# Decoder layer on one core: the values from the unshifted x in the first pass, the index queries in the second

## The chip, the cores and the metric

The kernel runs on one core of one Trainium2 chip. TensorE (PE) multiplies, VectorE (DVE) and ScalarE (ACT) work element by element, GpSimd (POOL) and SyncE (SP) here issue nearly nothing but transfers (DMA). The metric is the device time of one execution in microseconds (us); lower is better.

## The reference

One decoder layer on x of 512 tokens x 2048 channels, with a condition c of 2048 numbers. What matters here:

```python
mod = silu(c) @ w_ada + b_ada                     # 6 x 2048 numbers
sh1, sc1, gt1, sh2, sc2, gt2 = split(mod, 6)
h = rmsnorm(x, g_mix) * (1 + sc1) + sh1
proj = h @ w_in       # q_a k_a v_a, q_b k_b v_b, qi, ki, wi, g_a, g_b
y_a = stick_breaking_attention(q_a, k_a, v_a) @ w_a         # 8 heads
y_b = dsa_attention(rope(q_b), rope(k_b), v_b, rope(qi), rope(ki), wi) @ w_b
x = x + (1 + gt1) * ((sigmoid(g_a) * y_a + sigmoid(g_b) * y_b) @ w_o)
h = rmsnorm(x, g_ffn) * (1 + sc2) + sh2
x = x + (1 + gt2) * conv_ffn(h, w_up, conv_w, conv_b, w_down)
return rmsnorm(x, g_final)
```

v_a has 1024 columns, qi 1024 (16 heads of 64). The norm of a token is one number, 1/rms, so for the unshifted s = x * g_mix * (1 + sc1) one has h = s / rms + sh1 and h @ w = (s @ w) / rms + sh1 @ w.

## The kernel before

Every large product is made of three fp32r matmuls of a high and a low half (`mm3`, L178 to L180: high by high, high by low, low by high). Weights come by SP into a ring of 8 tiles `raw` (`load`, L153 to L155); ACT makes their high half `wh` (L168), DVE the low half `wl` (L170), in three rooms. x and h are cut into 16 tiles of 128 channels (KT), counted by k. Tiles of 128x512 come from a ring of 62 (`slot`, named F), small working tiles from pairs named `w`, `T`, `ta`, `sp`, and one tile of 128x1280 is named `soft`. PSUM has three `acc` banks, four `att` and one `outs`. Each engine runs its instructions in a fixed order, which a scheduler made from the code; `behind(...)` pins an instruction after another.

mod is made in 160 halves (`ada_half`): a load of 512 KB of w_ada by SP (L320) and a product with a sum on DVE (L321, 128x1024). They are strewn over the program.

Pass 1 (loop at L397) makes 7 of the 8 query tiles from s: in each of 16 steps two halves of sc1, one tile of x, its square for the norm (L394), s in high and low (ACT, and DVE at L418), one weight tile and 21 matmuls of 512 columns. In its last step come the norm: four pairs of small matmuls (L368), the root, the spread over all partitions (L379) and its copy (L424). Pass 2 (L463) makes, in each of 16 steps, h of tile k (L437, L438, cast L466, low half L468), two halves of sh1 for the next tile, and 24 matmuls into eight tiles of values. Behind it come the tail columns (ki, wi), the eighth query tile (`w_qi7`) from h, and two tiles of the other columns.

Since the seven query tiles lack the shift and the norm, these come later. 31 units (`unit`, 168 matmuls of 256 columns each, a Strassen-like product of 2 x 2 blocks) make the other columns. In each, `between` is called twice and advances the tasks of `beside` by a step: tables of the rotary functions, `shift_queries` (sh1 @ w_qi, from w_qiT on DVE at L610, with diagonal matrices spread by PE at L596), and `index_ropes` (for each query tile: load, times 1/rms at L647, plus the shift at L648, rotary), and after these halves of mod in `soft`, one in a step. A second half of mod is taken in each unit at the second call. In the stick-breaking heads, `some_ada(2)` stands in each head. The units of w_o (u = 0 to 7) take one half of mod each, and behind u = 6 `some_ada(len(ada_left))` issues whatever is left of the 160. L1104 to L1112 are in that loop; the last unit (u = 7) has the second norm's work in it. Then come the units of w_up and w_down.

Of the kernel before, what the change touches and what calls it, by code (L numbers as in the profile page):

```python
# [10 lines left out]
F32 = mybir.dt.float32  # L11
# [65 lines left out]
def block_kernel(ctx: ExitStack, tc: tile.TileContext, A: dict, out: bass.AP):  # L77
# [284 lines left out]
    def rms(squares, blocks=range(NQB), bank=outs):  # L362

        total = bank()
        at = slice(blocks[0] * P, (blocks[-1] + 1) * P)
        for b in blocks:
            for i, t in enumerate(squares):
                mm(total[:, b : b + 1], t[:, b * P : (b + 1) * P], ones[:, :1], start=b == blocks[0] and i == 0,  # L368
                   stop=i == len(squares) - 1, skip_group_check=True)
        r = sb.tile([P, NQB], F32, tag="r", bufs=2, name=nm("r"))  # L370
        rb = r[:, blocks[0] : blocks[-1] + 1]
        act(rb, total[:, blocks[0] : blocks[-1] + 1], AF.Sqrt, scale=1.0 / D, bias=eps)
        nc.vector.reciprocal(rb, rb)
# [5 lines left out]
        mm(out[:, at], ones, wide[:, at], start=True, stop=True)  # L379
        yield out  # L380


    xt, total = [], None
    qi_ps = [acc() for _ in range(3)] + [att() for _ in range(4)]
    norm = None

    def next_x():
        x = slot()
# [5 lines left out]
            tt(total, total, sq, ALU.add)  # L394
        return total or sq

    for k in range(KT):  # L397
        if k == 6:
            past = t2k("w", 2)[:, :P]
            with behind(pins["load"]):  # L400
                nc.sync.dma_start(const, A["consts"][:, :5])
                nc.sync.dma_start(past, A["consts"][:, 5])
            nc.gpsimd.tensor_copy(mask[0], ident)
            nc.gpsimd.tensor_copy(mask[1], past)
# [6 lines left out]
        if k == KT - 1:  # L411
            norm = rms([total])
            next(norm)
        ada_end(t, t + 1)
        stt(amp[:, 0, k : k + 1], mod[:, t : t + 1], 1.0, g_mix[:, k : k + 1], ALU.add, ALU.mult)
        h0 = slot(F32R), slot(F32R)
        act(h0[0], x, AF.Copy, scale=amp[:, 0, k : k + 1])
        stt(h0[1], x, amp[:, 0, k : k + 1], h0[0].bitcast(F32), ALU.mult, ALU.subtract)  # L418
        w = prep(A["w_qi"][k], NQ * P)
        for j in range(NQ):  # L420
            mm3(qi_ps[j], cols(w, j), h0, k == 0, k == KT - 1)
            if k == KT - 1 and j == 0:
                rstd = t2k("T", 2)
                act(rstd, next(norm), AF.Copy)  # L424
# [30 lines left out]
    pv = None

    def ada_tile(k):
        last = [ada_half(cb, k, half) for half in range(2)][1]
        ada_end(k, k + 1)
        return last  # L460

    ada_tile(0)
    for k in range(KT):  # L463
        modulate(xt[k], k, 0, xt[k])
        hi, lo = slot(F32R), slot(F32R)
        act(hi, xt[k], AF.Copy)  # L466
# [10 lines left out]
        for i in range(8):  # L477
            mm3(pv[i], cols(h[k], i % 4), cols(w, i // 4, S), k == 0, k == KT - 1)
        if k in EARLY:
            forms_late(EARLY.index(k))  # L480
    for i in range(8):
        save(vd[i], evac(pv[i]))
# [12 lines left out]
    save(td_tail[:TN], evac(ps, slice(0, TN))[:TN])  # L495

    xd = dram("xd", 64)
    for j, (src, dst) in enumerate(((A["w_qi7"], qid[7]), (A["w_x0"][0], xd[0]), (A["w_x0"][1], xd[1]))):
        ps = (acc, att)[j % 2]()
        for c in range(2):  # L500
            w = prep(src[c])
            for k in range(8):
                i = 8 * c + k
                last = mm3(ps, cols(w, k), h[i], i == 0, i == KT - 1)
                if j == 2 and k % 2:
# [78 lines left out]
            save(rope_d[n], o)  # L584

    rope_d = dram("rope", 2, 2 * S)
    corr = macc[:, : 2 * NQ, :].rearrange("p (j a) b -> p j (a b)", a=2)

    def shift_queries():

        rows = [t2k(tag, 2) for tag in ("w", "T") for _ in range(2)]
        diag = None
        for i in range(5):
            if i:
                ps = outs()
                mm(ps, ones, diag, start=True, stop=True)  # L596
                act(rows[i - 1], ps, AF.Copy)
            if i < 4:
                diag = t2k("ta", 2)
                for b in range(4):  # L600
                    ts(diag[:, b * P : (b + 1) * P], ident, mod[:, 4 * i + b : 4 * i + b + 1], None, ALU.mult)
                yield
        for j in range(NQ):
            for half in range(2):
                w = sb.tile([P, 1024], F32, tag="soft", name=nm("soft"))
                nc.sync.dma_start(w, A["w_qiT"][j, :, half * 1024 : (half + 1) * 1024])
                for i in range(2):
                    at = w[:, i * S : (i + 1) * S]
                    n = 2 * half + i
                    stt(at, at, 1.0, rows[n], ALU.mult, ALU.mult, accum_out=corr[:, j, n : n + 1])  # L610
                yield
        tt(corr[:, :, :2], corr[:, :, :2], corr[:, :, 2:], ALU.add)
        tt(corr[:, :, 0], corr[:, :, 0], corr[:, :, 1], ALU.add)
# [18 lines left out]
    def index_ropes():  # L632

        tabs = [t2k("T", 2) for _ in range(2)]
        for i, t in enumerate(tabs):
            save(t, rope_d[1][:, i * S : (i + 1) * S])
        rstd = t2k("w", 2)
        save(rstd, rd)
        for j in range(9):
            r = t2k("w", 2)  # L640
            soft = sb.tile([P, 10 * P], F32, tag="soft", name=nm("soft"))
            tmp = soft[:, :S], soft[:, S : 2 * S]
            if j < 8:
                save(r, qid[j])
                yield
                if j < NQ:
                    tt(r, r, rstd, ALU.mult)  # L647
                    act(r, r, AF.Identity, bias=corr[:, j, 0:1])  # L648
                    yield
# [233 lines left out]
    for hd in range(NH):  # L883
# [632 lines left out]
def _layout(i):  # L1516
# [102 lines left out]
```

## Time and profile before

| | |
|---|---|
| Times of three runs | 2747.16, 2744.15, 2747.07 us (median 2747.07) |
| Profiled execution | 2744.77 us, of which the span is 2742.9 (1.87 us lie around it) |
| PE busy | 2678.6 us, 98% of the span |
| DVE busy | 2409.0 us, 88% |
| ACT busy | 1450.6 us, 53% |
| POOL busy | 314.2 us, 11% |
| Mean granted clock of PE | 0.995 |

Pass 1 lies at 13.5 to 98 us, pass 2 at 101.6 to about 190, the units from 236 to 860, the stick heads from 905 to about 1100, the units of w_o from 1247 to 1411. A row of a timeline gives start and length in us, engine, line, operation, what it writes and reads with shapes, and in brackets how long the engine had been idle and what ended that. A row of waits gives who waited for whom, the sum in us, how many times, and the longest.

### The profile page before, as it was taken

To read this page: it belongs to the slowest core of one execution; us is meant where nothing else is said; L and a number is where in the kernel's file an instruction comes from. 1 tells how busy PE (TensorE), PEld (TensorE's weight loads), DVE (VectorE), ACT (ScalarE), POOL (GpSimd) and SP (SyncE) were. 2 spreads that over 40 slices of the span, in tenths; PEclk is the share of its full clock that TensorE was granted. 3 is DMA by queue.
4 is the path that set the end of the run, shared out by engine and by line. 5 is a ranking of instruction groups with operands and counts; after the bars stand their busy time and mean duration, and the time that the engine had idled before them with its cause. 6 is when DMAs were issued, how large, how long until landed. Compare 5 with 4: busy or idle time off the path is not lost. (4 is left out here: it accounts for less than half of the span.)

```text
span 2742.9 us, 47708 instructions
## 1 busy us (share of the span) xinstructions
PE 2678.6 (98%) x18704; PEld 2449.0 (89%) x18704; DVE 2409.0 (88%) x3452; ACT 1450.6 (53%) x2045; POOL 314.2 (11%) x519
## 2 busy tenths in 40 slices
PE   8999999999999999999999999999999999999996
PEld 6779999999998777889999999999999998888875
DVE  8978989988897899788888999999999997888876
ACT  4444454455556665434466555555555455546452
POOL 0010000001002011111220100000000001012112
PEclk9999999999999999999999999999999999999998
DMA  9973456755566458866773566666665436559686
GB/s 339 363 258 123 163 177 207 234 178 185 173 209 222 137 190 279 270 222 190 229 254 114 173 185 177 182 181 178 183 177 166 137 123 234 169 158 257 192 243 188
DMA packets 164189, 550.08 MB, mean 201 GB/s; under 512 B 21414, under 2 KB 21798, under 8 KB 163964
## 3 DMA queue, kind: packets, MB, share of 16 engines
q1 hardware_dynamic: 116220, 405.34, 44.7%
q0 software_dynamic: 47152, 141.30, 18.4%
q8 instruction: 147, 2.41, 0.3%
q14 instruction: 78, 0.64, 0.1%
q10 hardware_dynamic: 592, 0.39, 0.0%
HBM read 453.71 MB, written 89.83 MB: 198 GB/s over the span
## 5 line engine op out<-in xcount | busy, mean ns | idle before, releaser
L168 ACT ACTIVATE wh<-raw 128x1024 fp32r<-128x1024 f32 (+2 forms) x792 | 828.1, 1053 | 942.4 <-DVE raw L272 180.0
L170 DVE TENSOR_TENSOR wl<-raw,wh 128x1024 fp32r<-128x1024 f32 (+2 forms) x792 | 953.3, 1211 | 123.4 <-ACT wh L168 115.4
L178 PE MATMUL acc<-F,wh 128*128 128x256 f32 (+1 forms) x2464 | 706.9, 289 | 15.2 <-ACT wh L168 10.7
L180 PE MATMUL acc<-F,wl 128*128 128x256 f32 (+1 forms) x2464 | 706.8, 287 | 5.4 <-DVE wl L170 5.4
L179 PE MATMUL acc<-F,wh 128*128 128x256 f32 (+1 forms) x2464 | 707.4, 287 | 0.0
L178 PE MATMUL att<-F,wh 128*128 128x256 f32 (+1 forms) x2448 | 700.1, 288 | 5.2 <-DVE sp L308 4.2
L180 PE MATMUL att<-F,wl 128*128 128x256 f32 (+1 forms) x2448 | 700.5, 286 | 2.1 <-DVE wl L170 2.1
L179 PE MATMUL att<-F,wh 128*128 128x256 f32 (+1 forms) x2448 | 701.1, 286 | 1.2 <-DVE F L199 1.2
L178 PEld LDWEIGHTS acc<-F,wh 128*128 128x128 f32 x2464 | 462.4, 188 | 33.0 <-ACT wh L168 15.2
L180 PEld LDWEIGHTS acc<-F,wl 128*128 128x128 f32 x2464 | 462.7, 188 | 16.4 <-DVE wl L170 6.8
L178 PEld LDWEIGHTS att<-F,wh 128*128 128x128 f32 x2448 | 459.7, 188 | 18.0 <-issue 5.6
L179 PEld LDWEIGHTS acc<-F,wh 128*128 128x128 f32 x2464 | 463.1, 188 | 11.0 <-DVE F L418 0.9
L179 PEld LDWEIGHTS att<-F,wh 128*128 128x128 f32 x2448 | 459.7, 188 | 12.7 <-DVE F L199 4.3
L180 PEld LDWEIGHTS att<-F,wl 128*128 128x128 f32 x2448 | 459.6, 188 | 11.0 <-DVE wl L170 2.9
L321 DVE SCALAR_TENSOR_TENSOR raw<-raw,raw 128x1024 f32<-128x1024 f32 x155 | 185.7, 1218 | 0.0
L178 PE MATMUL att<-wh,F 128*128 128x512 f32 x448 | 178.3, 398 | 0.2 <-ACT wh L168 0.2
L179 PE MATMUL att<-wl,F 128*128 128x512 f32 x448 | 174.8, 390 | 0.0
L180 PE MATMUL att<-wh,F 128*128 128x512 f32 x448 | 174.8, 391 | 0.0
L268 DVE TENSOR_TENSOR raw<-raw,raw 128x1024 f32<-128x1024 f32 x80 | 97.5, 1218 | 39.6 <-DMA raw<-in_w_x 22.3
L179 PE MATMUL acc<-wl,F 128*128 128x512 f32 x288 | 113.8, 395 | 4.4 <-DVE wl L170 4.4
L178 PE MATMUL acc<-wh,F 128*128 128x512 f32 x288 | 112.5, 393 | 1.1 <-ACT wh L168 0.9
L180 PE MATMUL acc<-wh,F 128*128 128x512 f32 x288 | 112.8, 392 | 0.0
(360 smaller groups left out, 3620.7 us busy)
## 6 DMA issues: line engine op xcount, KB each, us to landing
raw<-in_w_up SPq DMA_DIRECT2D x164, 512.0 KB, 3.6
raw<-in_w_ada SPq DMA_DIRECT2D x155, 512.0 KB, 5.4
raw<-in_w_x SPq DMA_DIRECT2D x128, 512.0 KB, 4.3
raw<-in_w_down SPq DMA_DIRECT2D x104, 512.0 KB, 5.0
xd<-F POOLq DMA_DIRECT2D x64, 256.0 KB, 2.8
F<-xd POOLq DMA_DIRECT2D x64, 256.0 KB, 5.0
raw<-in_w_o SPq DMA_DIRECT2D x32, 512.0 KB, 5.3
soft<-in_w_gate SPq DMA_DIRECT2D x32, 512.0 KB, 4.1
```

The lines of the kernel that those rows point to most:

```text
L168: pins["wh"] = act(wh, raw, AF.Copy)
L170: pins["wl"] = tt(wl, raw, wh.bitcast(F32), ALU.subtract)
L178: mm(ps, ah, bh, start=first, stop=False, skip_group_check=not check)
L179: mm(ps, ah, bl, start=False, stop=False, skip_group_check=not check)
L180: return mm(ps, al, bh, start=False, stop=last, skip_group_check=not check)
L268: last_v = tt(s, a21, a22, ALU.add)
L321: return stt(raw, raw, 1.0, cb[half], ALU.mult, ALU.mult, accum_out=macc[:, t, half : half + 1])
```

## The change

Pass 1 now makes the eight value tiles from s (24 matmuls a step). Its last two steps are ordered by hand so that the norm's matmuls stand between values, and two halves of sh1 move to its end. The values are copied from PSUM with 1/rms as ACT's scale in pass 2's first step and saved to `vd` in steps 4 to 11. Pass 2 makes all eight query tiles from h, so they need neither shift nor norm afterwards; the stage of the eighth tile is gone, `shift_queries` and the two corrections in `index_ropes` too. The values' shift row sh1 @ w_va is made by `shift_values` as the last task of `beside`: POOL loads half tiles of w_va, ACT scales their rows by sh1, POOL adds them up in DRAM by accumulating transfers, two matmuls with ones add over partitions, and eight accumulating transfers add the row to the value tiles in `vd`. Rotary tables and mask are loaded behind the tail, not in pass 1. The tasks of `beside` have 53 steps instead of 58, so 9 halves of mod go through `soft` instead of 4; heads 1 to 6 take one half each, 6 instead of 16; behind u = 6 of w_o 5 more halves are left than before.

```diff
-NQ = 7
+NQ = 8
...
+def evac(ps, rows=slice(0, P), scale=None):
+    o = slot()
+    act(o[rows], ps[rows], AF.Copy, **({} if scale is None else {"scale": scale}))
...
+def value(i, k):
+    mm3(pv[i], cols(h0[k], i % 4), cols(wv[k], i // 4, S), k == 0, k == KT - 1)
 for k in range(KT):
...
-        w = prep(A["w_qi"][k], NQ * P)
-        for j in range(NQ):
-            mm3(qi_ps[j], cols(w, j), h0, k == 0, k == KT - 1)
-            if k == KT - 1 and j == 0:
-                rstd = t2k("T", 2)
-                act(rstd, next(norm), AF.Copy)
+        wv.append(prep(A["w_va"][k]))
+        if k < KT - 2:
+            for i in range(8):
+                value(i, k)
...
+    ada_tile(0)
+    for i in range(1, 4):
+        value(i, KT - 2)
+    for k in range(KT - 2, KT):
+        value(0, k)
+    v0 = evac(pv[0])
+    norm = rms([total])
+    r_col = next(norm)
+    for i in range(4, 8):
+        value(i, KT - 2)
+    value(1, KT - 1)
+    rstd = t2k("T", 2)
+    act(rstd, next(norm), AF.Copy)
+    for i in range(2, 8):
+        value(i, KT - 1)
...
-    EARLY = (9,)
+    EARLY = (9, 13)
...
-        w = prep(A["w_va"][k])
+        w = prep(A["w_qi"][k])
         if k == 0:
-            for j in range(NQ):
-                save(qid[j], evac(qi_ps[j]))
-            pv = [outs()] + [acc() for _ in range(3)] + [att() for _ in range(4)]
+            act(v0, v0, AF.Copy, scale=r_col[:, :1])
+            vs = [v0] + [evac(pv[i], scale=r_col[:, i % 4 : i % 4 + 1]) for i in range(1, 8)]
+            qi_ps = [acc() for _ in range(3)] + [att() for _ in range(4)] + [outs()]
...
+        if 4 <= k < 12:
+            save(vd[k - 4], vs[k - 4])
+        for j in range(NQ):
+            mm3(qi_ps[j], cols(w, j), h[k], k == 0, k == KT - 1)
...
-    def shift_queries():
...
+    def shift_values():
+
+        def weights(k):
+            if k % 2:
+                both = sb.tile([P, 1024], F32, tag="soft", name=nm("soft"))
+                w = [both[:, i * S : (i + 1) * S] for i in range(2)]
+            else:
+                w = [t2k("T", 2) for _ in range(2)]
+            for i in range(2):
+                save(w[i], A["w_va"][k, :, i * S : (i + 1) * S])
+            return w
+
+        w = weights(0)
+        yield
+        for k in range(KT):
+            for i in range(2):
+                act(w[i], w[i], AF.Copy, scale=mod[:, k : k + 1])
+                save(v_sum[i], w[i], **({"accum_op": ALU.add} if k else {}))
+            if k + 1 < KT:
+                w = weights(k + 1)
+            yield
+        w = [t2k("T", 2) for _ in range(2)]
+        for i in range(2):
+            save(w[i], v_sum[i])
+        yield
+        for i in range(2):
+            ps = outs()
+            mm(ps, ones, w[i], start=True, stop=True)
+            act(w[i], ps, AF.Copy)
+            for b in range(NQB):
+                save(vd[4 * i + b], w[i], accum_op=ALU.add)
+            yield
...
-        rstd = t2k("w", 2)
-        save(rstd, rd)
...
-                if j < NQ:
-                    tt(r, r, rstd, ALU.mult)
-                    act(r, r, AF.Identity, bias=corr[:, j, 0:1])
-                    yield
...
-        for task in (rope_tables(), shift_queries(), index_ropes()):
+        for task in (rope_tables(), index_ropes(), shift_values()):
...
-            some_ada(2)
+            if 1 <= hd < NH - 1:
+                some_ada()
```

The order of instructions at three places. PE where pass 1 ends (L379 spreads the norm; `outs` and `acc` behind it are the first matmuls of pass 2). Before:

```order
L178 MATMUL att_110<-F_771,wh_67 128x512
L379 MATMUL outs_783<-T_764,const 128x512
L179 MATMUL att_110<-F_772,wh_67 128x512
L180 MATMUL att_110<-F_771,wl_70 128x512
L178 MATMUL outs_876<-wh_73,F_840 128x512
L179 MATMUL outs_876<-wl_76,F_840 128x512
```

and in the change:

```order
L178 MATMUL att_111<-wh_67,F_776 128x512
L179 MATMUL att_111<-wl_70,F_776 128x512
L180 MATMUL att_111<-wh_67,F_777 128x512
L379 MATMUL outs_837<-T_816,const 128x512
L178 MATMUL outs_922<-F_885,wh_73 128x512
L179 MATMUL outs_922<-F_886,wh_73 128x512
L178 MATMUL acc_915<-F_885,wh_73 128x512
```

L379 stood ahead of two matmuls of pass 1 and stands behind all of them now; the second matmul of pass 2 now reads the low half of h (F_886), where before it read the high half and the weights' low half.

POOL in the units while `shift_values` runs (in the change's numbering L613 loads a half tile of w_va, L621 accumulates in DRAM, L701 saves a unit's results, which is L685 before; what each waits for is in brackets, DMASW followed by a number being the landing of an earlier transfer). In the change:

```order
L701 DMA xd_1767<-F_5996 128x512 [waits Activation_49]
L701 DMA xd_1768<-F_5997 128x512 [waits Activation_49]
L621 DMA v_sum_2006<-T_6003 128x512 [waits DMASW3_49,Activation_49]
L621 DMA v_sum_2007<-T_6004 128x512 [waits DMASW4_49,Activation_49]
L613 DMA T_6235<-in_w_va 128x512 [waits DMASW3_49]
L613 DMA T_6236<-in_w_va 128x512 [waits DMASW4_49]
L621 DMA v_sum_2006<-soft_6170 128x512 [waits DMASW7_49,Activation_49]
L621 DMA v_sum_2007<-soft_6170 128x512 [waits DMASW0_49,Activation_49]
L613 DMA soft_6402<-in_w_va 128x512 [waits DMASW7_49,DMASW1_49,DMASW0_49]
L613 DMA soft_6402<-in_w_va 128x512 [waits DMASW2_49]
L701 DMA xd_1769<-F_6228 128x512 [waits Activation_49]
L701 DMA xd_1770<-F_6229 128x512 [waits Activation_49]
```

A unit had the two saves alone here; now two pairs of accumulates and two pairs of loads stand between them and the next two, and each pair of loads waits for the accumulates just ahead of it.

SP between units 6 and 7 of w_o (L154 loads weights, L320 a half of w_ada). Before:

```order
L154 DMA raw_14087<-in_w_o 128x1024
L320 DMA raw_14220<-in_w_ada 128x1024
L154 DMA raw_14326<-in_w_o 128x1024
L154 DMA raw_14328<-in_w_o 128x1024
L154 DMA raw_14330<-in_w_o 128x1024
L154 DMA raw_14332<-in_w_o 128x1024
```

and in the change:

```order
L154 DMA raw_14094<-in_w_o 128x1024
L320 DMA raw_14227<-in_w_ada 128x1024
L320 DMA raw_14322<-in_w_ada 128x1024
L320 DMA raw_14325<-in_w_ada 128x1024
L320 DMA raw_14328<-in_w_ada 128x1024
L320 DMA raw_14331<-in_w_ada 128x1024
L320 DMA raw_14334<-in_w_ada 128x1024
L154 DMA raw_14348<-in_w_o 128x1024
L154 DMA raw_14350<-in_w_o 128x1024
L154 DMA raw_14352<-in_w_o 128x1024
L154 DMA raw_14354<-in_w_o 128x1024
```

Five more loads of w_ada stand ahead of unit 7's four weight tiles.

More of the change, by code (lines that the diff above doesn't have):

```diff
@@ L383, in block_kernel @@
     xt, total = [], None
-    qi_ps = [acc() for _ in range(3)] + [att() for _ in range(4)]
-    norm = None
+    pv = [outs()] + [acc() for _ in range(3)] + [att() for _ in range(4)]
     def next_x():
@@ L395, in next_x, with ada_tile @@
         return total or sq
+    def ada_tile(k):
+        last = [ada_half(cb, k, half) for half in range(2)][1]
+        ada_end(k, k + 1)
+        return last
+    def evac(ps, rows=slice(0, P), scale=None):
+        o = slot()
+        act(o[rows], ps[rows], AF.Copy, **({} if scale is None else {"scale": scale}))
+        return o
+    h0, wv = [], []
+    def value(i, k):
+        mm3(pv[i], cols(h0[k], i % 4), cols(wv[k], i // 4, S), k == 0, k == KT - 1)
     for k in range(KT):
         if k == 6:
-            past = t2k("w", 2)[:, :P]
             with behind(pins["load"]):
[L401 to L404, printed above, removed]
+                nc.sync.dma_start(const[:, :2], A["consts"][:, :2])
         t = KT + k
@@ L410, in block_kernel @@
         x = xt[k]
-        if k == KT - 1:
-            norm = rms([total])
-            next(norm)
         ada_end(t, t + 1)
         stt(amp[:, 0, k : k + 1], mod[:, t : t + 1], 1.0, g_mix[:, k : k + 1], ALU.add, ALU.mult)
-        h0 = slot(F32R), slot(F32R)
-        act(h0[0], x, AF.Copy, scale=amp[:, 0, k : k + 1])
-        stt(h0[1], x, amp[:, 0, k : k + 1], h0[0].bitcast(F32), ALU.mult, ALU.subtract)
-        w = prep(A["w_qi"][k], NQ * P)
-        for j in range(NQ):
-            mm3(qi_ps[j], cols(w, j), h0, k == 0, k == KT - 1)
-            if k == KT - 1 and j == 0:
-                rstd = t2k("T", 2)
-                act(rstd, next(norm), AF.Copy)
+        h0.append((slot(F32R), slot(F32R)))
+        act(h0[k][0], x, AF.Copy, scale=amp[:, 0, k : k + 1])
+        stt(h0[k][1], x, amp[:, 0, k : k + 1], h0[k][0].bitcast(F32), ALU.mult, ALU.subtract)
+        wv.append(prep(A["w_va"][k]))
+        if k < KT - 2:
+            for i in range(8):
+                value(i, k)
         for _ in range(2 if k == 8 else 1):
@@ L427, in block_kernel @@
                 total = next_x()
+    ada_tile(0)
[13 more added lines that the diff above has]
+        value(i, KT - 1)
     dram = lambda name, n, w=S: [dr.tile([P, w], F32, tag=f"{name}{i}", name=f"{name}{i}") for i in range(n)]
     save = nc.gpsimd.dma_start
-    qid, hd_, vd, rd = dram("qid", 8), dram("hd", KT // 2), dram("vd", 8), dram("rd", 1)[0]
-    save(rd, rstd)
+    qid, hd_, vd = dram("qid", NQ), dram("hd", KT // 2), dram("vd", 8)
     def modulate(x, k, which, h, at=slice(0, S)):
@@ L453, in forms_late @@
         form_u(f[p], xt[2 * p], xt[2 * p + 1])
[L455 to L462, printed above, removed]
+    vs = []
     for k in range(KT):
@@ L469, in block_kernel @@
         h.append((hi, lo))
[L470 removed]
+        w = prep(A["w_qi"][k])
         if k == 0:
[L472 to L474 removed]
+            act(v0, v0, AF.Copy, scale=r_col[:, :1])
+            vs = [v0] + [evac(pv[i], scale=r_col[:, i % 4 : i % 4 + 1]) for i in range(1, 8)]
+            qi_ps = [acc() for _ in range(3)] + [att() for _ in range(4)] + [outs()]
         if k % 2 == 0:
             save(hd_[k // 2], xt[k])
[L477 to L478 removed]
+        if 4 <= k < 12:
+            save(vd[k - 4], vs[k - 4])
+        for j in range(NQ):
+            mm3(qi_ps[j], cols(w, j), h[k], k == 0, k == KT - 1)
         if k in EARLY:
             forms_late(EARLY.index(k))
[L481 to L482 removed]
+    for j in range(NQ):
+        save(qid[j], evac(qi_ps[j]))
     TN = IDXD + IDXH
@@ L497, in block_kernel @@
     xd = dram("xd", 64)
-    for j, (src, dst) in enumerate(((A["w_qi7"], qid[7]), (A["w_x0"][0], xd[0]), (A["w_x0"][1], xd[1]))):
+    past = t2k("w", 2)[:, :P]
+    nc.sync.dma_start(const[:, 2:], A["consts"][:, 2:5])
+    nc.sync.dma_start(past, A["consts"][:, 5])
+    nc.gpsimd.tensor_copy(mask[0], ident)
+    nc.gpsimd.tensor_copy(mask[1], past)
+    for j, (src, dst) in enumerate(((A["w_x0"][0], xd[0]), (A["w_x0"][1], xd[1]))):
         ps = (acc, att)[j % 2]()
@@ L504, in block_kernel @@
                 last = mm3(ps, cols(w, k), h[i], i == 0, i == KT - 1)
-                if j == 2 and k % 2:
+                if j == 1 and k % 2:
                     p = i // 2
@@ L586, in block_kernel @@
     rope_d = dram("rope", 2, 2 * S)
-    corr = macc[:, : 2 * NQ, :].rearrange("p (j a) b -> p j (a b)", a=2)
-    def shift_queries():
[L591 to L613, printed above, removed]
@@ L1553, in _layout @@
     qi = sec(6)
-    a["w_qi"] = asc(qi[:, : NQ * P]).reshape(KT, P, NQ * P)
-    a["w_qiT"] = asc(qi[:, : NQ * P].T).reshape(NQ, P, D)
-    a["w_qi7"] = tiles(qi[:, NQ * P :])[0]
+    a["w_qi"] = asc(qi).reshape(KT, P, NQ * P)
     tn = IDXD + IDXH
```

7 lines of the change are left out of this document (2 added, 5 removed).

## The prediction

> **What bounds the kernel now.** I read the page's busy shares first, then the windows by stage, then in each stage the waits of PE.
>
> ```profile
> PE 2678.6 (98%) x18704; PEld 2449.0 (89%) x18704; DVE 2409.0 (88%) x3452; ACT 1450.6 (53%) x2045; POOL 314.2 (11%) x519
> 13.00:95.00 82.00, 79.27 (x334) 62.78 (x335) 78.43 (x143) 35.19 (x48) 0.59 (x2) 1.00 0.94 348
> 95.00:185.00 90.00, 86.89 (x369) 70.66 (x368) 80.61 (x141) 44.34 (x59) 8.77 (x16) 0.96 0.90 332
> 185.00:235.00 50.00, 50.00 (x222) 39.36 (x221) 31.68 (x55) 27.65 (x50) 5.98 (x11) 1.00 0.36 121
> 255.00:352.00 97.00, 95.88 (x841) 95.42 (x840) 92.91 (x142) 40.54 (x50) 5.94 (x11) 1.00 0.50 164
> 1391.00:1411.00 20.00, 20.00 (x178) 19.95 (x176) 14.65 (x19) 11.32 (x17) 11.43 (x20) 1.00 0.92 281
> ```
>
> A window's row has its length, then busy time and count of PE, PEld, DVE, ACT and POOL, then granted clock, DMA share and GB/s. PE is busy for all but 64 us of the span of 2742.9. Work removed from other engines is therefore worth nothing by itself; only a PE wait that goes or comes counts. The change keeps PE's matmuls but for a handful, so the sum is one of waits. Of these the first window has more than its idle 2.7 us shows: DVE is busy 78.4 of 82 there, back to back, and sets the step:
>
> ```profile
> 78.02 1.22 DVE L321 SCALAR_TENSOR_TENSOR raw<-raw,raw 128x1024 f32<-128x1024 f32 x1
> ...
> 80.79 1.09 DVE L170 TENSOR_TENSOR wl<-raw,wh 128x896 fp32r<-128x896 f32 x1
> ...
> 83.07 1.22 DVE L321 SCALAR_TENSOR_TENSOR raw<-raw,raw 128x1024 f32<-128x1024 f32 x1
> ...
> 95.67 0.39 PE L180 MATMUL att<-F,wl 128*128 128x512 f32 x1
> 95.90 0.39 PE L179 MATMUL att<-F,wh 128*128 128x512 f32 x1
> ```
>
> DVE's step is 83.07 - 78.02 = 5.05 us. A matmul of 512 columns starts 0.23 us after the one before (50 / 222 = 0.225 in the third window), so the 21 of a step need 4.73 to 4.83 us: PE loses some 0.28 us in a step.
>
> **The change part by part.** *Pass 1* gets 24 matmuls a step, 5.45 us. DVE's step grows by the difference of a full L170 (1.22, in the rows of w_o below) and the 1.09 above, to 5.18. It no longer sets the pace, and 16 x 0.28 = 4.5 us go. The loads of a step (x 256 KB, two adas of 512, the weights) grow from 1728 to 1792 KB, or 337 GB/s over 5.45 us, below the 348 that the first window reached. The 48 matmuls that the last query tile had as a stage of its own are in pass 2 now, so PE's work over both passes and the tail is the same.
>
> *The gap between the passes* is to be covered by 18 matmuls that the code puts behind the norm. But by PE's order the matmul that spreads the norm (L379) has come to stand last in pass 1, behind all values, so ACT's copy, the modulation and the cast still follow with PE empty:
>
> ```profile
> 97.03 1.02 PE L379 MATMUL outs<-T,const 128*128 128x512 f32 x2
> 98.09 0.60 ACT L424 ACTIVATE T<-outs 128x512 f32<-128x512 f32 x1 [4.82 <-PE outs L379]
> 98.79 0.69 DVE L437 TENSOR_TENSOR w<-F,T 128x512 f32<-128x512 f32 x1 [0.59 <-ACT T L424]
> 99.53 1.54 ACT L438 ACTIVATE F<-w,mod,amp 128x512 f32<-128x512 f32 x2
> 100.97 0.61 ACT L466 ACTIVATE F<-F 128x512 fp32r<-128x512 f32 x1
> 101.64 0.80 PE L178 MATMUL outs<-wh,F 128*128 128x512 f32 x1 [3.11 <-ACT F L466]
> ```
>
> Before, one matmul (L180 at 98.13) stood in this gap; now none, and PE's second matmul needs the low half of h, which DVE makes after two L321 (2 x 1.22). I add 1.0 us, with 0 and 2.4 as bounds. Pass 2 and the tail had DVE at 80.6 of 90 us; the second early forms (the 13 beside 9) and the scaled evacuations on ACT (44 of 90) fit beside PE and I cost them at nothing; the hd, vd and qid transfers on POOL (8.8 of 90) too. If the cover goes, the scaled copies (0.60 each, as L424) keep acc and att from the first queries, 1 to 2 us. Together: -4.5 + 1.0 = **-3.5** (bounds -5 and -1).
>
> *The 31 units behind the passes.* The waits of PE from 236 to 860 and their causes:
>
> ```profile
> PE att L178 <- DVE sp L308: 3.5, 5, 2.1
> PE acc L180 <- DVE wl L170: 3.4, 2, 2.7
> ...
> DVE w L647 <- DMA w<-qid: 5.6, 3, 2.1
> 807.62 1.22 DVE L321 SCALAR_TENSOR_TENSOR soft<-soft,raw 128x1024 f32<-128x1024 f32 x1 [2.02 <-DMA soft<-in_w_ada]
> 811.00:814.00 3.00, 3.00 (x16) 3.00 (x16) 2.49 (x3) 0.00 (x0) 0.00 (x0) 0.50 0.70 249
> L596 PE MATMUL outs<-ta,const x8: 590/590/591, 397.3 to 425.3; 128*128 128x512 f32 x8
> ```
>
> (a) Eight L596 rows of 0.59 us go, four of the new ones-matmuls come: -2.4 at most, I take -2.0. (b) In the index ropes DVE stood three times, 5.6 us, before L647 for a query tile, because rstd held one of two w buffers; L647 and that holder go, the tile is read a step ahead, and with it the first row's 3.5 us: -3.5. (c) The first ada of soft came while the last rope tile held soft, DVE waited 2.0 and PE 2.7, and the clock was halved for 3.0 us behind it. Now soft is free for long before: -2.7 - 1.5 = -4.2. The 28 DVE products L610 (0.68 each) that leave had cover from PE and give nothing. Sum **-9.7**; bounds -12 and -3, the latter if the other DVE order of these units makes waits of its own.
>
> *The shift row of the values* is new on POOL, ACT and the DMA queues in these units: for each of 32 half tiles a scale on ACT (0.60 as L424, hidden where ACT has 40.5 of 97), an accumulate in DRAM and a load, four of each in a unit, over eight units. The nearest rows are the accumulates of L1251, 256 KB in pairs:
>
> ```profile
> L1251 POOL DMA_DIRECT2D sumd<-F x2: 897/1042/1188, 2387.8 to 2388.4; - x2
> DMA to landing us min/median/max: 3.8/5.5/7.2
> ...
> L1251 POOL DMA_DIRECT2D sumd<-F x2: 851/984/1118, 2466.1 to 2466.7; - x2
> DMA to landing us min/median/max: 4.0/6.1/8.1
> L685 POOL DMA_DIRECT2D xd<-F x62: 542/542/566, 255.0 to 848.8; - x62
> F<-xd POOLq DMA_DIRECT2D x64, 256.0 KB, 5.0
> 2380.00:2400.00 20.00, 20.00 (x89) 16.31 (x88) 14.94 (x17) 8.49 (x10) 1.79 (x2) 1.00 0.68 200
> ```
>
> By POOL's order every load waits for the landing of the accumulate that frees its buffer, and the next accumulate stands behind it, so the chain is serial. With issues of 0.9 and 0.54 and a second accumulate that lands after 7.2 us, a pair takes 0.9 + 7.2 + 0.54 = 8.6 us; a unit has two pairs and two saves: 2 x 8.6 + 1.1 = 18.3 us, where PE's unit is 168 x 0.1133 = 19.04 (178 in 20 us, last window above is of the same kind). It just holds. Where it doesn't, ACT waits in order at L620 with its casts (wh) behind it, and PE behind them. At 8.1 us the unit takes 20.1: 1.1 over in each of eight units is 9. A load has half a unit, 9.5 us, to its use and lands in 5.0 (the row F<-xd), so a lead of some 5 covers the first part of that and 4 remain. Between 0 (at 7.2) and 4 I take **+1.5** (bounds 0 and, without the lead, +9).
>
> The Trainium skill ("DMA: Bandwidth & Descriptors", section "Anatomy of one DMA — SWDGE (gpsimd) path") fits such a transfer with 2.0 us plus bytes over 436 KB per us, an estimated 2.6 us for 256 KB; the rows above have 3.8 to 8.1. By the fit the term would be 0 and the time 1.5 us less; I go by the rows, since a plain transfer isn't an accumulate.
>
> *Stick heads.* Ten adas of 1.3 us leave DVE's 100.9 of 115 us there, but PE loses little:
>
> ```profile
> 905.00:1020.00 115.00, 114.22 (x515) 82.74 (x514) 100.93 (x239) 70.11 (x108) 18.52 (x36) 1.00 0.56 185
> 1030.00:1036.00 6.00, 4.09 (x15) 2.30 (x14) 6.00 (x13) 3.52 (x10) 0.00 (x0) 1.00 0.05 10
> ```
>
> PE's idle is 0.8 and 1.9 us: **-1.5** (bounds -3 and 0).
>
> *What is left over.* Nine adas leave by soft instead of four, six in the heads instead of sixteen, so five are left, and all are issued at once behind unit 6 of w_o (`some_ada(len(ada_left))`), ahead of unit 7's weights on SP and on DVE. Here is that place before:
>
> ```profile
> 1378.49 1.43 SPq L154 DMA_DIRECT2D raw<-in_w_o  x2
> ...
> 1383.38 1.23 DVE L268 TENSOR_TENSOR raw<-raw,raw 128x1024 f32<-128x1024 f32 x1 [1.10 <-DMA raw<-in_w_o]
> 1384.52 1.22 DVE L170 TENSOR_TENSOR wl<-raw,wh 128x1024 fp32r<-128x1024 f32 x1
> 1385.66 0.18 DVE L338 TENSOR_TENSOR mod<-mod,vec 128x32 f32<-128x32 f32 x1
> ...
> 1386.42 0.43 DVE L309 TENSOR_TENSOR F<-sp,ta 128x256 f32<-128x256 f32 x1
> 1386.76 1.22 DVE L170 TENSOR_TENSOR wl<-raw,wh 128x1024 fp32r<-128x1024 f32 x1
> ...
> 1390.63 0.28 PE L178 MATMUL att<-F,wh 128*128 128x256 f32 x1
> raw<-in_w_ada SPq DMA_DIRECT2D x155, 512.0 KB, 5.4
> ```
>
> The L170 at 1384.52 is unit 6's last, that at 1386.76 unit 7's first, which PE needs from 1390.9. The sixth ada load now waits for the ring's eighth buffer, which that last L170 frees; three more L321 (3.7 us) stand ahead of it on DVE against 2.5 of wait and L268 that no longer do, so it ends near 1387. Load issue 0.3 and landing 3.9 to 5.4: 1391 to 1392.7. Its L321 (1.3), L309 and L312 (0.43 each), L337 and L338 (0.18 each) and the L170 (1.2) end at 1394.7 to 1396.4. PE stands 4 to 5.5 us; with the two residual products, L268 and L314 ahead of the next L170 it stands some 2 more, and 1 at the third. At 811 above a stop of 2.7 us was followed by half clock for 3 us: 1.5 more. Sum 7 to 10; I take **+8** (bounds +5 and +11.5).
>
> **Sum.** -3.5 - 9.7 + 1.5 - 1.5 + 8 = -5.2, against the profiled execution's 2744.77: 2739.6. That execution is near the low end of the runs (2744.15), the median lies 2.3 above it; I say **2740**.
>
> **The rivals.** (1) *The refill is hidden.* If the sixth ada's buffer comes free earlier or PE's queue has other matmuls, the +8 goes: 2731.6. For it: DVE was idle 1.1 us at 1383. Against: the order on SP and DVE is fixed, and unit 7's loads left at 1378.49 before. (2) *Slower: the accumulate chain saturates.* From a landing of 7.5 us on, a POOL unit is longer than 19.04. At 9 us it is 2 x 10.4 + 1.1 = 21.9, 2.9 over, times eight 23; less the lead of 5, PE loses 18 instead of 1.5: 2756. For it: the queues are in use 0.50 of the time there (window 255 to 352), and to that come 1 MB of loads and 1 MB of accumulates, which read and write, in each unit. Against: 7.2 at a share of 0.68 in the nearest place. (3) *The units' waits only move:* another order of DVE's work makes PE wait elsewhere, and -9.7 shrinks to -3: 2746.3. For it: DVE at 92.9 of 97, where a late cast can't be made up. Against: more DVE work leaves these units than comes. That the covering of the norm doesn't happen is in the forecast; if it did, 3 us more would go.
>
> **How the numbers follow.** Forecast 0.45, refill hidden 0.20, saturated chain 0.14, waits moved 0.21. What the runs can tell from no change is 0.2%, 5.5 us: 2741.6 to 2752.6 counts as the same. The forecast's own range is 2735 to 2745, of which I count 0.27 as faster and 0.18 as same; rival 1 is faster, rival 2 slower, rival 3 same but for 0.02 on each side. Faster 0.49, same 0.35, slower 0.16. The range reaches from rival 1, with a little for its own terms, to just short of rival 2: 2730 to 2752.
>
> **What would show it.** Pass 1: a step of 5.45 us on PE, without waits for ACT's or DVE's F; the gap of 3.1 us before L178 is there, and grown. Units: no PE wait on L308 in the rope units, none at the first soft ada. Shift row: the time from issue to landing of the accumulates, under or over 7.5, and whether ACT waits for `T<-in_w_va`. w_o: a PE wait of 4 to 6 us on L170 at the start of unit 7. A PE wait above 2 us at any other place, or no wait at unit 7, would make the prediction wrong.

## The result

The changed kernel takes 2764.38 us (median of four runs, 2760.50 to 2768.88) against 2747.11 before (2744.15 to 2747.28): 1.0065 times as long, with a 95% interval of 1.0051 to 1.0079. The forecast was 2740 with a range of 2730 to 2752, so it had the wrong sign. The profiled execution took 2760.50, with a span of 2758.7, the low end of its runs.

PE's busy time and its count of matmuls are nearly as before (2678.6 us and 18704); what has grown is its idle time, from 64 to 78 us. The page's first row after:

```profile
PE 2680.3 (97%) x18700; PEld 2454.8 (89%) x18700; DVE 2386.3 (87%) x3369; ACT 1466.7 (53%) x2067; POOL 368.4 (13%) x591
```

Where it went shows when the start of the same PE matmul is read in both traces. The lag is the start after minus the start before; from the first unit on the matmuls correspond one to one, but for the eight of L596 that went and the four with ones that came.

| Stretch, by the times before | Lag at its end | Change in it | Forecast |
|---|---|---|---|
| to the first unit (235.4) | -5.6 | -5.6 | -3.5 |
| units 1 to 30 (to 825.2) | +5.9 | +11.5 | -9.7 + 1.5 = -8.2 |
| stick heads and w_b (to 1247) | +2.5 | -3.5 | -1.5 |
| w_o up to unit 6 (to 1382) | +4.6 | +2.2 | 0 |
| between units 6 and 7 and in unit 7 (to 1422) | +17.5 | +12.8 | +8 |
| behind it, to the end of the span | +15.8 | -1.7 | 0 |

So the forecast held to within 5 us in all stretches but one, the units. There the loss of each unit (its length, from its first matmul to the next unit's, minus the 19.04 of an undisturbed one) sorts by the task beside it:

| Task beside the units | Loss before | Loss after |
|---|---|---|
| rotary tables (units 1 to 8) | 4.2 | 5.1 |
| shift of the queries (9, 10) | 4.0 | none |
| index ropes (17 to 27; now 9 to 17) | 5.8 | 4.1 |
| first ada in soft (30; now 28) | 4.6 | 0.9 |
| shift row of the values (now 18 to 27) | none | 20.0 |
| sum | 18.6 | 30.1 |

The last but one row is what the forecast gave 1.5 us, beside two products with ones that cost 0.9 each. Units 18 to 25 lose 12.1 of the 20.0, unit 26 alone 6.9. Three views of the changed kernel show it. First the windows of that stretch (length, busy and count of PE, PEld, DVE, ACT, POOL, clock, DMA share, GB/s), the second of them from the kernel before in a block of its own:

```profile
562.00:745.00 183.00, 172.94 (x1498) 170.72 (x1496) 137.84 (x157) 101.63 (x139) 58.03 (x84) 1.00 0.88 246
```

```profile
562.00:745.00 183.00, 178.98 (x1567) 178.03 (x1566) 161.97 (x194) 104.80 (x141) 16.25 (x30) 1.00 0.56 177
```

Then, after, what PE and what DVE wait for between 562 and 745 us (in us, times, longest):

```profile
PE att L178 <- DVE sp L308: 5.3, 3, 1.9
PE acc L178 <- DVE sp L308: 3.5, 4, 1.3
PE acc L180 <- DVE wl L170: 0.8, 1, 0.8
```

```profile
DVE raw L268 <- DMA raw<-in_w_x: 34.0, 9, 6.6
```

and the time from issue to landing, there, of the units' weights (L154) and of the accumulates (L621):

```profile
DMA to landing us min/median/max: 3.7/5.9/10.2
...
DMA to landing us min/median/max: 4.3/7.0/10.8
```

By the prediction's mechanism PE would wait for ACT's casts, which stand behind L620. ACT does stand at L620 in this stretch, six times in units 22 to 25 ("issue" is a wait whose end the profile doesn't show):

```profile
ACT soft L620 <- DMA soft<-in_w_va: 10.9, 5, 4.8
ACT soft L620 <- issue: 4.4, 1, 4.4
```

But only one of the resulting late casts reaches PE, by the 0.8 us for L170 above. All else that PE waits for is L308, DVE's evacuation of a product. L308 stands on DVE behind L268, the next unit's sum of two weight tiles, and L268 waits for these. Two units of the changed kernel side by side, unit 13 (from 467.5) beside the index ropes and unit 20 (from 603.8) beside the shift row, DVE's rows:

```profile
477.32 0.69 DVE L644 TENSOR_TENSOR soft<-soft,T 128x512 f32<-128x512 f32 x1
478.07 1.22 DVE L170 TENSOR_TENSOR wl<-raw,wh 128x1024 fp32r<-128x1024 f32 x1
479.21 0.68 DVE L646 TENSOR_TENSOR w<-soft 128x512 f32<-128x512 f32 x1
479.82 1.22 DVE L170 TENSOR_TENSOR wl<-raw,wh 128x1024 fp32r<-128x1024 f32 x1
480.95 1.22 DVE L268 TENSOR_TENSOR raw<-raw,raw 128x1024 f32<-128x1024 f32 x1
482.09 0.41 DVE L308 TENSOR_TENSOR sp<-att,ta 128x256 f32<-128x256 f32 x1
...
613.60 1.22 DVE L170 TENSOR_TENSOR wl<-raw,wh 128x1024 fp32r<-128x1024 f32 x1
618.73 1.22 DVE L268 TENSOR_TENSOR raw<-raw,raw 128x1024 f32<-128x1024 f32 x1 [3.91 <-DMA raw<-in_w_x]
619.87 1.22 DVE L170 TENSOR_TENSOR wl<-raw,wh 128x1024 fp32r<-128x1024 f32 x1
621.00 0.42 DVE L308 TENSOR_TENSOR sp<-acc,ta 128x256 f32<-128x256 f32 x1
```

and PE's first row behind that:

```profile
621.57 0.36 PE L178 MATMUL acc<-F,wh 128*128 128x256 f32 x1 [1.32 <-DVE sp L308]
```

In both units SP issues the later of the two tiles 7.9 us behind the unit's start. In unit 13 DVE comes to L268 at 13.5, behind other work and without a wait. In unit 20 it is there at 11.1, waits 3.9, and L268 starts at 15.0; L308 is over 1.3 us too late. So in the order of unit 20 L268 may begin up to about 13.5 us behind a unit's start at no cost, which leaves a weight tile 13.5 - 7.9 = 5.6 us from issue to landing. (In unit 13 a cast, L170, stands ahead of L268 that unit 20 has between L268 and L308; there it could begin some 1.1 us later.) In units 18, 20 and 22 the tile landed 6.1, 6.9 and 6.6 us behind its issue. Between 410 and 545 us, beside the index ropes, the same row of L154 stays under that:

```profile
DMA to landing us min/median/max: 3.4/4.2/5.0
```

Unit 26 has the longest of these stops. Its L268 waited 6.6 us for a tile; in this unit the loads that read `v_sum` back, two saves, an ada, the unit's weights and the first accumulates into `vd` lie close together. Runs 1 and 9 below have these accumulates too and lose 0.9 us there, so they alone aren't the cause. PE then waited 3.3 us for L308, and its clock was halved behind that, which is some 2.8 of the unit's 6.9 us by the length of the stretch at half clock (746.6 to 753.4, with PE at work from 747.7):

```profile
747.00:753.00 6.00, 5.26 (x24) 5.29 (x25) 4.85 (x7) 0.93 (x2) 0.57 (x1) 0.50 0.94 242
```

The second loss, at unit 7 of w_o. The timeline of the changed kernel, SP's rows, then DVE's, then PE's:

```profile
1371.99 15.18 SPq L320 DMA_DIRECT2D raw<-in_w_ada  x6
1387.98 6.42 SPq L154 DMA_DIRECT2D raw<-in_w_o  x4
...
1390.00 1.23 DVE L321 SCALAR_TENSOR_TENSOR raw<-raw,raw 128x1024 f32<-128x1024 f32 x1 [2.04 <-DMA raw<-in_w_ada]
...
1395.10 0.42 DVE L308 TENSOR_TENSOR sp<-acc,ta 128x256 f32<-128x256 f32 x1
...
1397.45 1.22 DVE L170 TENSOR_TENSOR wl<-raw,wh 128x1024 fp32r<-128x1024 f32 x1
...
1395.67 0.55 PE L178 MATMUL acc<-F,wh 128*128 128x256 f32 x1 [2.97 <-DVE sp L308]
1410.74 1.87 PE L1070 MATMUL att<-const,T 128*128 128x1 f32 x8 [4.34 <-DMA T<-soft]
```

Five adas stand ahead of unit 7's weights on SP and ahead of unit 6's last evacuations on DVE. PE waits 3.0 us for L308, and in unit 7 another 4.3 us for a sum of squares that POOL accumulates into a T tile: unit 6's results, from which the squares are made, came late too. Two windows behind these waits show a clock of 0.72 and 0.54 on the mean:

```profile
1394.00:1400.00 6.00, 4.33 (x26) 4.36 (x27) 6.00 (x14) 1.64 (x2) 0.37 (x1) 0.72 1.02 407
...
1410.00:1416.00 6.00, 5.26 (x26) 5.26 (x27) 0.49 (x1) 0.00 (x0) 4.61 (x10) 0.54 0.95 291
```

### The profile page after: what moved, and what is told of

The parts are those of the page before. It is cut to its first block, busy times and chain, and to the rows that moved or that the text cites. A ratio compares the mean times of both kernels' runs of the same rounds, so it can differ in the third digit from the quotient of the medians.

```text
span 2758.7 us, 47739 instructions
## 1 busy us (share of the span) xinstructions
PE 2680.3 (97%) x18700; PEld 2454.8 (89%) x18700; DVE 2386.3 (87%) x3369; ACT 1466.7 (53%) x2067; POOL 368.4 (13%) x591
## 4 chain that ended last, share of the span: by engine, by line
PE 76%; DVE 9%; DMA 7%; issue 6%; ACT 1%; POOL 1%; SPq 0%; DVEq 0%; POOLq 0%; ACTq 0%
PE att L180 12%; PE att L178 12%; PE att L179 12%; PE acc L180 10%; PE acc L178 10%; PE acc L179 10%; DVE wl L170 3%; DMA raw<-in_w_x 1%; PE acc L862 1%; DMA v_sum<-T 1%; PE outs L179 1%; PE outs L180 1%; PE outs L178 1%; PE acc L768 1%; DMA raw<-in_w_down 1%
## 5 line engine op out<-in xcount | busy, mean ns | idle before, releaser
L168 ACT ACTIVATE wh<-raw 128x1024 fp32r<-128x1024 f32 (+1 forms) x790 | 827.5, 1055 | 921.1 <-DVE raw L272 172.4
L170 DVE TENSOR_TENSOR wl<-raw,wh 128x1024 fp32r<-128x1024 f32 (+1 forms) x790 | 952.1, 1212 | 126.3 <-ACT wh L168 117.9
L178 PE MATMUL att<-F,wh 128*128 128x256 f32 (+1 forms) x2448 | 703.8, 288 | 11.1 <-DVE sp L308 7.8
L178 PEld LDWEIGHTS acc<-F,wh 128*128 128x128 f32 x2448 | 460.9, 188 | 30.1 <-ACT wh L168 10.0
L180 PEld LDWEIGHTS att<-F,wl 128*128 128x128 f32 x2448 | 461.2, 188 | 12.8 <-DVE wl L170 4.9
L321 DVE SCALAR_TENSOR_TENSOR raw<-raw,raw 128x1024 f32<-128x1024 f32 x150 | 179.6, 1217 | 3.3 <-DMA raw<-in_w_ada 3.3
L268 DVE TENSOR_TENSOR raw<-raw,raw 128x1024 f32<-128x1024 f32 x80 | 97.3, 1216 | 59.8 <-DMA raw<-in_w_x 39.8
```

Of the source, the lines that this page charges most:

```text
L168: pins["wh"] = act(wh, raw, AF.Copy)
L170: pins["wl"] = tt(wl, raw, wh.bitcast(F32), ALU.subtract)
L178: mm(ps, ah, bh, start=first, stop=False, skip_group_check=not check)
L180: return mm(ps, al, bh, start=False, stop=last, skip_group_check=not check)
L268: last_v = tt(s, a21, a22, ALU.add)
L321: return stt(raw, raw, 1.0, cb[half], ALU.mult, ALU.mult, accum_out=macc[:, t, half : half + 1])
```

## The experiments

A number behind each name is the median; the ratio, with its 95% interval, is to runs of the kernel before on the same chip (their medians were 2744.19, 2745.69 and 2746.29 in the three groups). The change itself has 1.0065.

**1. The accumulates left out.** In `shift_values`:

```diff
-                save(v_sum[i], w[i], **({"accum_op": ALU.add} if k else {}))
+                if not k:
+                    save(v_sum[i], w[i])
```

> The change, but the shift row's accumulating transfers are left out from the second step on (the first tile's row alone is added to the values); the loads of w_va and ACT's scales stay. The units lose 18 us between 563 and 773 us in the change's trace (units 18 to 27, the two matmuls with ones taken off). If the accumulates are the cause, by whatever road, this goes: 2764.4 - 16 = about 2748, PE's waits in these units under 4 us, DMA share there below 0.75. If the loads and ACT's place in the order (L620 ahead of the casts) are the cause, it stays above 2758.

Measured: 2759.07, 1.0056 (1.0041 to 1.0071). By its time this is the second case, above 2758; the 5.3 us less than the change are not clear of the noise, since the intervals of the two ratios overlap. The trace has something of both cases. The window, DVE's waits and the landing of the weights in the stretch:

```profile
562.00:745.00 183.00, 176.93 (x1542) 175.28 (x1541) 146.61 (x166) 105.29 (x143) 30.71 (x55) 1.00 0.67 211
```

```profile
DVE raw L268 <- DMA raw<-in_w_x: 27.2, 9, 4.5
```

```profile
DMA to landing us min/median/max: 3.4/4.3/6.8
```

The median landing is that of a quiet stretch again, yet L268 still waits 3.0 us on the mean and units 18 to 28 still lose 12.6 us (20.9 in the change's trace). What is left are the loads of w_va by POOL, and ACT's scales.

**2. ACT's scale left out.**

```diff
-                act(w[i], w[i], AF.Copy, scale=mod[:, k : k + 1])
```

> The change without ACT's scale by sh1 (the sum is that of the unscaled weights); loads and accumulates stay, so POOL's chain is the same but ACT waits for nothing of it. Theory share: the accumulates fill the DMA queues (share 0.89 to 0.95), the units' own weights land late, DVE waits for them at L268 with L308 behind it, and PE waits for L308: nothing changes, 2760 to 2766, DVE's wait for in_w_x at L268 between 563 and 773 us stays near 35 us. Theory chain (the prediction's): the loss comes through ACT standing at L620 for a load: it goes, about 2748.

Measured: 2795.49, 1.0187 (1.0171 to 1.0202), which fits neither. Without the scale the scheduler let POOL's chain run ahead of the units in its order, and put the first load of an ada into `soft` 26 rows, some five units, earlier in SP's queue. That load waited for the chain to let go of `soft`, with the units' weights behind it; PE stood for 43.3 us in one place (its waits, and SP's timeline, which has no row between 614 and 674):

```profile
PE att L180 <- DVE wl L170: 43.3, 1, 43.3
```

```profile
674.12 0.33 SPq L320 DMA_DIRECT2D soft<-in_w_ada  x1
674.55 0.38 SPq L320 DMA_DIRECT2D raw<-in_w_ada  x1
675.03 8.98 SPq L154 DMA_DIRECT2D raw<-in_w_x  x4
```

So its time says nothing on ACT's part. Ahead of that place its trace does. In units 18 to 20 ACT has nothing of the chain to do, and they still lose 7.0 us (4.6 in the change), with PE waiting for L308 as there (between 560 and 628 us):

```profile
PE acc L178 <- DVE sp L308: 3.3, 2, 3.1
PE att L178 <- DVE sp L308: 1.3, 1, 1.3
```

The scales are not needed for the loss. The run also measures the chain itself: free of ACT, the accumulates went from the pair at 567 to the one at 669 us in fourteen steps, 7.2 us a pair (7.6 over the first six, while weights were still being loaded). Two pairs of 7.6 and two saves (2 x 0.54) are 16.3 us, under a unit's 19.04. In the changed kernel they come 10.5 us apart (570.5 to 727.4 in fifteen steps), two to a unit. The chain ran late in its last units, as ACT's waits above show, but it isn't what PE waited for.

**3. No ada left over.** Eleven halves of mod in the heads instead of six.

```diff
-                some_ada()
+                some_ada(2 if hd < 6 else 1)
```

> The change with two halves of mod in heads 1 to 5 and one in head 6, eleven instead of six, so that none is left over behind unit 6 of w_o. Theory refill: the 12.8 us that the change loses at 1372 to 1422 us against before go, and some 2 of the 3.5 that the stick heads had gained: 2764.4 - 11 = 2753 (2751 to 2756). Rival: that loss comes from somewhere else (the residual, the norm's accumulates behind it): it stays, 2763 to 2766.

Measured: 2749.90, 1.0017 (1.0007 to 1.0027), 14.5 us less than the change, where 11 were expected. PE has no idle time between 1370 and 1410 us in that trace, and of the heads' gain of 3.5 us 3.1 stayed:

```profile
1370.00:1410.00 40.00, 40.00 (x352) 39.81 (x351) 34.13 (x44) 19.33 (x27) 16.13 (x26) 1.00 0.83 248
```

**4. Five adas left over in the kernel before.** Only the heads' count changes there.

```diff
-            some_ada(2)
+            some_ada(2 if hd < 3 else 1)
```

> The kernel before with eleven halves of mod in the stick heads instead of sixteen, so that five more are left behind unit 6 of w_o; nothing else changes. Theory refill: 12 us are lost between unit 6 and the end of unit 7, and up to 2 gained in the heads: 2747.1 + 11 = 2758 (2755 to 2760). Rival as in the kernel with heads refilled: no change, 2745 to 2748.

Measured: 2756.26, 1.0050 (1.0033 to 1.0066), 12.1 us more. The two waits of the changed kernel appear in this one, in which nothing else was touched:

```profile
PE att L1053 <- DMA T<-soft: 5.7, 1, 5.7
PE acc L178 <- DVE sp L308: 2.9, 1, 2.9
```

With 3 this settles the refill: 12.1 and 14.5 us, what the heads' count moves included, and its cause.

**5. L268 behind L308.** In `unit`, for all units:

```diff
-        last_v = tt(s, a21, a22, ALU.add)
+        with behind(*([pins["u3"]] if "u3" in pins else [])):
+            last_v = tt(s, a21, a22, ALU.add)
...
-        tt(u3, r2, p1, ALU.add)
+        pins["u3"] = tt(u3, r2, p1, ALU.add)
```

> The change with one order edit: DVE's sum of two weight tiles for the next unit (L268), which stood ahead of L308, is pinned behind L308 in all units. Loads, accumulates and the DMA share stay. Theory place: what PE waits for between 563 and 773 us is L308 behind L268 behind a late weight tile, so 8 to 12 us go (2752 to 2756), although the weights land as late as before (median 5.9). Rival (bandwidth or ACT at L620 as such): the lateness only shows up in the next product, nothing is won, 2761 to 2767.

Measured: 2754.76 (2746.38 to 2761.55), 1.0031 (1.0017 to 1.0046): 9.6 us less than the change, as theory place has it. But its profile (an execution of 2760.13, at the high end of the ten) does not show that gain. PE's waits for L308 are gone in the stretch, and others have come, for casts behind the late tiles:

```profile
PE acc L178 <- ACT wh L168: 5.2, 2, 3.6
PE acc L180 <- DVE wl L170: 1.8, 3, 0.8
PE att L180 <- DVE wl L170: 0.8, 2, 0.5
```

Units 18 to 20 lose nothing (4.6 in the change), units 21 to 24 lose 13.2 (5.4), and units 18 to 28 together 19.3 (20.9). The larger gain is elsewhere: `unit` also makes w_o, where PE's waits for L308 up to unit 6 are gone, so that 2.2 us are won on the kernel before in place of the 2.2 lost. Against that stands a new wait at 871 us with half clock behind it, 4.2 us in all:

```profile
PE outs L750 <- DMA F<-tail: 2.6, 1, 2.6
```

So in this trace a late weight tile that no longer holds L308 costs nearly as much at its next use, and the 9.6 us of the medians are not located.

**6. Both edits (3 and 5).**

> The order edit (L268 behind L308) together with eleven halves of mod in the heads. If the two losses are separate they add: 2749.9 - 10 = 2740 (2737 to 2744). If not, it stays at 2747 to 2752.

Measured: 2742.96, 0.9986 (0.9976 to 0.9996): the two gains add, by 7 us where 10 were expected. The wait at L750 is in this trace too (2.4 us).

**7. The shift row summed by DVE.** One load of 512 KB by SP a step, and two DVE instructions into a held pair of T tiles, in the place of POOL's loads, ACT's scales and the accumulates into `v_sum`:

```diff
+        total = [t2k("T", 2) for _ in range(2)]
...
-                act(w[i], w[i], AF.Copy, scale=mod[:, k : k + 1])
-                save(v_sum[i], w[i], **({"accum_op": ALU.add} if k else {}))
+                if k:
+                    stt(total[i], w[i], mod[:, k : k + 1], total[i], ALU.mult, ALU.add)
+                else:
+                    ts(total[i], w[i], mod[:, k : k + 1], None, ALU.mult)
```

> The change with the shift row summed by DVE in two T tiles (32 instructions of 128x512, 0.7 us each, four in a unit) from 512 KB loads by SP into soft; ACT's scales, POOL's loads and the accumulates into v_sum go, the eight accumulates into vd stay. Theory late weights: the share falls to about 0.7 and DVE's work stands ahead of L268 as in the rope units; units 18 to 25 lose less than 3 us instead of 12: 2764.4 - 12 = 2752 (2749 to 2755). Rival: DVE, four instructions fuller, becomes the bound, 2760 or more.

Measured: 2742.45, 0.9983 (0.9968 to 0.9997), 21.9 us less than the change, where 12 were expected: I had left out unit 26's 6.9 us, of which 4.8 went with the rest. The edit also takes out the step that read `v_sum` back, so one more half goes through `soft` and four are left over, not five; the refill is 10.2 us in this trace, 2.6 less. The stretch has no PE idle at all, with a DMA share of 0.74 and DVE fuller than in any other run:

```profile
562.00:745.00 183.00, 183.00 (x1603) 181.89 (x1602) 172.76 (x207) 90.10 (x118) 18.45 (x29) 1.00 0.74 225
```

**8. The shift row by DVE, and no ada left over (7 and 3).**

> The shift row summed by DVE, and eleven halves of mod in the heads: 2749.9 - 12 = 2738 (2735 to 2742), faster than before, if both losses are what they seem; otherwise 2745 to 2752.

Measured: 2730.06 (2727.75 to 2733.11), 0.9939 (0.9924 to 0.9954), 8 us below what was expected, since run 7's edit had given 21.9 and not 12. This beats both kernels, by 0.6% and 1.2%.

**9. No transfers of the shift row.** The loop does its first step alone:

```diff
-            for i in range(2):
-                act(w[i], w[i], AF.Copy, scale=mod[:, k : k + 1])
-                save(v_sum[i], w[i], **({"accum_op": ALU.add} if k else {}))
-            if k + 1 < KT:
-                w = weights(k + 1)
+            if not k:
+                for i in range(2):
+                    act(w[i], w[i], AF.Copy, scale=mod[:, k : k + 1])
+                    save(v_sum[i], w[i])
```

> The change with the loads, scales and accumulates of the shift row left out behind the first tile (the values lack the other fifteen tiles' shift); the steps, DVE's order in the units (L268 ahead of L308) and all else stay. Without the accumulates alone 12.6 us were still lost in units 18 to 28, 7.9 of them in 18 to 25. Theory late weights: with no transfers of the shift row left the share falls to about 0.5, and units 18 to 25 lose under 1.5 us: 2759.1 - 7 = 2752 (2749 to 2754). Rival order: these units are short of DVE work between the loads and L268, so DVE comes to L268 before any normal landing: 5 to 8 us of the loss stay there, 2756 to 2760.

Measured: 2746.47, 0.9997 (0.9987 to 1.0008), 17.9 us less than the change, more than expected. Units 18 to 25 lose 1.2 us, with DVE's order as in the change:

```profile
562.00:745.00 183.00, 182.08 (x1595) 180.95 (x1594) 153.09 (x170) 90.76 (x120) 17.43 (x30) 1.00 0.60 177
```

```profile
DVE raw L268 <- DMA raw<-in_w_x: 14.7, 9, 3.5
```

L268 waits here too, but 1.6 us on the mean, which the 13.5 us above allow. So DVE's early arrival costs nothing by itself; the loss takes late weights. Runs 1 and 9 part the traffic: of 20.9 us lost in units 18 to 28 in the change, 12.6 remain with the loads and scales alone and 4.1 (1.8 of them the matmuls with ones) with none.

**10. The shift row ahead of the index ropes** (on top of 8).

```diff
-        for task in (rope_tables(), index_ropes(), shift_values()):
+        for task in (rope_tables(), shift_values(), index_ropes()):
```

> The kernel with the shift row on DVE and eleven halves in the heads, with the tasks of the units in the order rotary tables, shift row, index ropes (as the kernel before had them), so that the tables saved to DRAM are not read back at once. Theory: the 3 to 4.5 us that unit 9 loses with DVE at L638 waiting for the table go: 2730.1 - 3.5 = 2726.5 (2724.5 to 2728.5). Rival: the wait moves to the first rope unit wherever that is, 2729 to 2732.

Measured: 2731.47, 0.9943 (0.9931 to 0.9956), no different from 8. The rival's number came, but not its mechanism: unit 9's loss fell from 3.2 to 1.6 us and DVE waited only 0.4 us for the tables in the first rope unit, yet the rope units, now units 18 to 26, lose 5.6 where all but the first had lost none; DVE waits for L268 there again, 17.8 us in nine times.

## Why the prediction was wrong

- **Pass 1 and the gap (forecast -3.5, measured -5.6): right in kind.** PE has no idle time left in pass 1 and the gap has grown, as two views after show, the windows of pass 1 and pass 2 and the waits of PE from 13 to 236 us:

```profile
13.00:95.00 82.00, 81.96 (x355) 67.19 (x355) 80.06 (x141) 34.81 (x45) 1.11 (x1) 1.00 0.97 360
95.00:185.00 90.00, 85.59 (x372) 69.85 (x372) 81.65 (x148) 48.97 (x65) 9.52 (x17) 0.98 0.90 321
```

```profile
...
PE outs L178 <- ACT F L474: 3.5, 1, 3.5
PE outs L179 <- DVE F L476: 0.9, 1, 0.9
```

The 0.9 us for the low half had been set at 1.0. By the starts of the matmuls, the thirteen steps from the second on took 65.7 us before, where their matmuls alone take 13 x 4.76 = 61.9, and 70.7 after, which is 13 x 5.44 and nothing more. So 3.8 us went, where 13 x 0.28 = 3.6 were said, but not by 0.28 in each step: before, the first four of these steps ran without a loss and later ones took up to 5.94, when a cast came late. The forecast left out the clock: behind the gap it was halved for 6.8 us before and for 3.4 after (0.96 and 0.98 on the mean of 95 to 185 us), which is worth some 1.7 us. That part of the gain is luck.

- **The units' waits (forecast -9.7, measured -6.7): right in kind.** L596 gave -2.2 (-2.0 said) and the first ada in soft -3.7 (-4.2 said). The index ropes gave -1.7 (-3.5 said). Their eight inner units lose nothing now, but the first one reads back the tables that the task ahead has just saved, and loses 4.1; the order of the tasks before had parted the two. The tables' units cost 0.9 more. In run 10 the old order took most of this wait away, and late weight tiles in the rope units came in its place.

- **The shift row (forecast +1.5, measured 20.0 - 1.8 = +18.2): this step failed,** and with it the sign. It priced the accumulates by POOL's serial chain, with ACT at L620 as the way to PE, and asked only whether that chain fits into a unit. It does, by run 2. The accumulates landed in 7.0 us in the median (7.2 had been taken) and 10.8 at most, ACT stood at L620 for 15.3 us, and PE lost 0.8 by it. The step had the DMA share in hand (0.50, to which loads and accumulates come), but used it for the accumulates' own landing and not for that of the weights, which went from 4.4 to 5.9 us in the median (562 to 745 us). The place is L268 on DVE. Before's trace already had that wait, in DVE's waits from 236 to 860 us, and at little cost to PE:

```profile
DVE raw L268 <- DMA raw<-in_w_x: 22.3, 15, 3.2
```

  It had some 5.6 us from issue to landing to spend. The work that left DVE in these units has at most a small part: DVE comes to L268 at 11.1 us of a unit instead of 13.5, which by run 9 costs nothing, and the cast that now stands between L268 and L308 takes some 1.1 us of the room. No run has late tiles with the old order, so that part isn't measured. Rival 2 (saturated chain) had about the price, +18, by a mechanism that cost PE 0.8 us.

- **The stick heads (forecast -1.5, measured -3.5): beyond the bound of -3.** Run 3 shows that eleven adas there cost little against six (3.1 of the 3.5 us stay).

- **The refill (forecast +8, measured +12.8, above the bound of +11.5): right in kind, the place half right.** PE did stop at unit 7 because the left-over adas stand ahead of its weights. It stopped first for L308 of unit 6, behind its L321, and not for L170. The term left out the sums of squares: 4.3 us more. The half clock came twice, not once.

- What stays open: why w_o's first units lose 2.2 us (0.8 in run 3). PE waits for L308 there, 3.3 us in place of 1.2, and run 5, which moves L268, has none of these waits; why the tiles come later there wasn't looked into. The loads of w_va and the accumulates were not parted further than by run 1. Behind unit 7 the lag grew by another 2.0 us (a wait at 1537 us with half clock behind it) and fell again near the end; nothing was run on that.

## What to carry to other kernels

When a change adds transfers, the first question is not whether the new chain keeps up but which wait for an existing transfer has how much slack: read, for each load that an in-order engine waits for, its time from issue, the landing now, and what stands behind the waiting instruction. An engine that comes to such a wait early loses nothing by that; what counts is whether the tile lands within the slack. A count that decides what is "left over" for a later place is part of the change, and it is cheap to pay it where an engine has cover: here 14 us for one line.

## What the runs showed that was not expected

- With loads and scales but no accumulates (run 1) the median landing of the units' weights was 4.3 us, as without any (4.3 in run 9), and PE still lost 6.1 of 183 us against 0.9. The median hides it: what counts is the one tile on which L268 stands, whose wait went from 1.6 to 3.0 us on the mean.
- A DMA share of 0.74 cost PE nothing (run 7) and one of 0.67 cost 6 us (run 1). The share says less than when the one tile lands that L268 needs: issued 7.9 to 8.0 us behind the start of units 18, 20, 22 and 24, it landed at 12.3 to 12.6 in run 7 and at 13.1 to 14.2 in run 1, where 13.5 is the limit in run 1's order.
- Taking away an instruction (run 2) made the kernel 31 us slower, because the scheduler's order of a third engine's queue hung on it.
- DVE at 172.8 of 183 us busy was no bound (run 7): its 32 added products fell into waits.
